# Two-layer transformer block, float32: long convolutions by transforms at odd frequencies, even and odd samples apart, with the upper half of the filter products on GpSimd

## Chip, cores and metric

One core of a Trainium2 chip. The time is device microseconds of one execution; before and after are compared by the median of runs. The engines: TensorE (PE in the profile, its weight loads PEld), VectorE (DVE), ScalarE (ACT), GpSimd (POOL), SyncE (SP), which only issues DMAs here. SBUF is the on-chip memory that all engines read, PSUM the memory into which TensorE writes.

## What is computed

A diffusion transformer of width 1024 on 256 latent tokens (x) and 256 context tokens (ctx), in float32. Two layers, each: feed-forward, mixer, feed-forward, every one behind a norm whose scale and shift come from a modulation (a product of the conditioning vector with a large matrix, `mod_w`). The first layer's mixer has two halves of 512 channels: differential attention, and a Hyena branch with two long convolutions. The second layer's mixer is neighbourhood attention. The change is in the Hyena branch:

```
def long_conv_bidir(v, h_fwd, h_bwd, skip):
    n = v.shape[1]
    taps = jnp.concatenate([h_fwd, jnp.zeros_like(h_fwd[:1]), h_bwd[:0:-1]], axis=0)
    taps_f = jnp.fft.rfft(taps.astype(jnp.float32), n=2 * n, axis=0)
    v_f = jnp.fft.rfft(v.astype(jnp.float32), n=2 * n, axis=1)
    y = jnp.fft.irfft(v_f * taps_f[None], n=2 * n, axis=1)[:, :n]
    return (y + v.astype(jnp.float32) * skip.astype(jnp.float32)).astype(v.dtype)
...
    z = x1 * long_conv_bidir(v, filt[:, 0, 0], filt[:, 0, 1], hy_b[0])
    z = x2 * long_conv_bidir(z, filt[:, 1, 0], filt[:, 1, 1], hy_b[1])
```

n is 256 and there are 512 channels. The branch runs for both streams, latent and context, with the same filters. The filters come from a small network of the position and a window.

## The kernel before

All activations are kept transposed, channels on partitions, 512 tokens wide (latent, then context). A float32 operand is split into a high and a low part (`split`, lines 154 to 157: ScalarE writes the high part, line 156, VectorE or GpSimd the low one, line 157), and a product is three matmuls (`mm3`, lines 159 to 162). So 160, 161, 162 are the lines of nearly all products, 156 and 157 those of nearly all splits; tiles are told apart by name.

The order of a run, with the times of the profile:

- To 64.7 us: loads, the first modulations on TensorE (`mod_group`, lines 247 to 274, weights `mw`, products at line 264, result `modT` at line 238), and the filters. `filter_taps` makes the windowed taps of a convolution as sums and differences of the two directions (`flt`). `filter_spectra` multiplies them with tables of cosines and sines: for each half `f` of the 256 frequencies a real and an imaginary part, each over two blocks of 128 taps; for the lower half there is a third product, for the frequency 256, which shares a row with the sine's frequency 0. ScalarE scales and copies the results, which go to memory (`TR`, `TI`, `TN`).
- 64.7 to 455 us: the first feed-forward. Its first block (`ffn_first`, `products`) needs the weights' splits (`wh`, `wl`) and the normed tokens `h`, which `Adaln.stream` makes: VectorE `xr` (line 487), ScalarE the high part (line 488), VectorE the low one (line 489). Its four results take all four tiles of the PSUM pool that the filters' spectra use too.
- 455 to about 706 us: the first mixer. Projections, attention heads (`head`), the Hyena inputs (`emit_hy`, with the short convolution and a transposition by line 779; v and x1 go to memory by tokens), per-head norms (`norms`), and the long convolutions, from 632 us. `spectrum` multiplies a stream's tokens (`vy`) with cosines and sines, two halves of the frequencies with a real and an imaginary part over two blocks of tokens: 24 matmuls of 512 columns. VectorE multiplies the results with the filter's parts (lines 824, 825), adds (line 826) and splits (`y`). `tn` takes the place of the real filter part in one product of the lower half. `conv1` goes back to tokens (24 matmuls), multiplies with x1 (line 843) and writes the result, `hz`, to memory, from where `load_tokens` takes it for the second convolution. `conv2` goes back to channels (48 matmuls of 256 columns for each stream) and multiplies with x2 (line 861).
- Then the output projection (`out_project`), over the attention's rows first (`za`), then over the convolution's (`zb`); a gated sum into the residual ends each product (line 515). Then the second feed-forward, and the second layer, to 1931 us.

The order on each engine is not that of the code: the framework's planner puts an instruction forward when its operands and buffers would be free, with the order of the code as the priority. So the profile has products of the attention's rows (`pd<-z`) between those of the convolutions, although they stand behind them in the code. Within an engine the order is then fixed.

Pools that the change touches: `fp`, three tiles for window, tables and filter parts; `tp`, ten tiles `T` of [128, 512]; `xp`, six tiles `X` of [128, 256], for norms, rotary embedding and x2. Filter parts are loaded by `load_filters` (lines 789 to 793) on SP's queue.

Of the kernel before, what the change touches and what calls it, by code (L numbers as in the profile page):

```python
# [10 lines left out]
F32 = mybir.dt.float32  # L11
# [7 lines left out]
P = 128  # L19
# [18 lines left out]
# columns of the small table of constants  # L38
_CO = {}
_n = 0  # L40
for _name, _w in (("ident", 128), ("sel", 8), ("row", 63), ("wf", 3), ("mask", 64)):
    _CO[_name] = slice(_n, _n + _w)
    _n += _w
# [3 lines left out]
def constants():  # L47
    """Tables that depend on shapes alone."""
# [11 lines left out]
    wf = np.full((P, 3), 2.0 / 512)  # L60
    wf[0] = 1.0 / 512, 2.0 / 512, 0.0
    cst[:, _CO["wf"]] = wf
    # Columns in reach of each query's column, in the order of the shifted bias (row 63 - c).
# [19 lines left out]
    # big: FC [2 chunks of 256], FS, FS^T, window [2 chunks of 512]  # L83
    tf = np.outer(np.arange(n), np.arange(n)) % 512
    th = tf * (2.0 * math.pi / 512)
    fc = np.cos(th)
    fs = -np.sin(th)
    fs[:, 0] = (-1.0) ** np.arange(n)
# [4 lines left out]
    rows = lambda m: m.reshape(2, P, -1).transpose(1, 0, 2).reshape(P, -1)  # L93
    dft = np.concatenate([rows(fc), rows(fs), rows(fs.T)], 1).astype(f32)
    return {"cst": cst, "rope": rope, "tmp": tmp, "dft": dft, "win": rows(win).astype(f32)}


class _K:
    """The state of the kernel being built."""
# [3 lines left out]
def tile_dit(ctx: ExitStack, tc: tile.TileContext, a: dict, out: bass.AP, dbg=None):  # L103
# [11 lines left out]
    xp = ctx.enter_context(tc.tile_pool(name="xp", bufs=6))  # L115
# [6 lines left out]
    # Pairs of [128, 512]: the two parts of a split operand, or two plain tiles.  # L122
# [31 lines left out]
    def split(hi, lo, src, eng=V):  # L154
        """src = hi + lo, each of 12 bits."""
        S.activation(hi, src, AF.Copy)  # L156
        eng.tensor_tensor(lo, src, hi.bitcast(F32), op=ALU.subtract)  # L157
# [12 lines left out]
    wf = cst[:, _CO["wf"]]  # L170
# [14 lines left out]
    # silu of the conditioning in two of 32 columns, which two is up to where a slice begins  # L185
# [39 lines left out]
    res = [big.tile([P, TOK], F32, name=f"res{d}") for d in range(NDC)]  # L225
# [9 lines left out]
    def mod_finish(l, batch, sums):  # L235
        """The bias, and from (chunk of a half, half, stream) to (half, chunk of a half, stream)."""
# [10 lines left out]
    def mod_group(l, batch, i, g):  # L247
        """A quarter of index i of a layer's modulation, on the tensor engine: 512 columns, half of the rows.
# [889 lines left out]
```

## Time and profile before

| | |
|---|---|
| runs | 1937.55, 1932.49, 1934.93 us, median 1934.93 us |
| span of the profiled execution, first to last instruction | 1931.2 us (no other time is listed for it) |
| TensorE matmul | 1880.6 us busy, 97% |
| TensorE weight loads | 1586.8 us, 82% |
| VectorE | 1253.9 us, 65% |
| ScalarE | 740.3 us, 38% |
| GpSimd | 72.3 us, 4% |
| granted TensorE clock, mean | 0.992 |

How to read what follows: a row of the timeline has the start in us, the duration in us, engine, line, operation, output and inputs by the program's names, shape and number; in brackets the idle time of the engine before it and what ended it. A row of the groups has line, engine, operation, names, shapes and number, then busy us, mean ns of one, idle us before and what ended that. Matmuls overlap, so that their pace is the distance of their starts and not their duration.

### The profile page before, as it was taken

The page shows a single profiled execution, that of the slowest core. Times are in us where ns is not written, and L with a number is a line of the kernel's source. Part 1 is how long each engine was busy: PE and PEld are TensorE (multiplying, and loading weights), DVE is VectorE, ACT ScalarE, POOL GpSimd, SP SyncE. Part 2 cuts the span into 40 slices and gives each one's busy share as a digit, 9 for nine tenths or more (in the row PEclk, how much of TensorE's full clock was granted, in tenths as well). Part 3 has the DMA queues.
Part 4 walks back from the last instruction along what each step waited for, and adds up shares of the span by engine and source line. Part 5 has one row for each costly group of instructions (what it writes and reads, how often), then busy time and mean ns, then how long its engine had stood idle before and what let it go on. Part 6 is the DMA issues. An engine that isn't in the chain of part 4 may idle for free.

```text
span 1931.2 us, 26004 instructions
## 1 busy us (share of the span) xinstructions
PE 1880.6 (97%) x10486; PEld 1586.8 (82%) x10486; DVE 1253.9 (65%) x1948; ACT 740.3 (38%) x1199; POOL 72.3 (4%) x63
## 2 busy tenths in 40 slices
PE   7999999999999999999999999999999999989998
PEld 3878788889877788888888888878889888889998
DVE  5557686666666785976775467763445654576665
ACT  4533233224556234232233242321233555554443
POOL 1000000000100001000000200000000000120000
PEclk9999999999999999999999999999999999989999
DMA  7674555451332322654464224642232333325552
GB/s 260 216 243 171 190 181 196 134 191 30 113 120 77 120 82 80 236 196 153 144 218 161 88 77 163 207 154 84 89 119 84 96 82 80 67 91 193 196 169 73
DMA packets 191153, 271.73 MB, mean 141 GB/s; under 512 B 19703, under 2 KB 139898, under 8 KB 191032
## 3 DMA queue, kind: packets, MB, share of 16 engines
q1 hardware_dynamic: 189468, 267.69, 42.5%
q10 hardware_dynamic: 1260, 2.14, 0.3%
q8 instruction: 82, 1.34, 0.3%
q14 instruction: 39, 0.32, 0.0%
q0 software_dynamic: 304, 0.24, 0.0%
HBM read 262.69 MB, written 7.34 MB: 140 GB/s over the span
## 4 chain that ended last, share of the span: by engine, by line
PE 57%; issue 11%; DVE 3%; DMA 2%; ACT 1%; POOL 1%; SPq 0%; POOLq 0%; DVEq 0%; ACTq 0%
PE pu L160 10%; PE pu L161 10%; PE pu L162 10%; PE pd L160 6%; PE pd L162 6%; PE pd L161 6%; PE ps L160 2%; PE ps L162 2%; PE ps L161 2%; DMA bias<-in_na_rpb_dram 2%; PE ps L672 1%; DVE wl L157 1%; DVE acc L444 1%; PE ps L298 1%; ACT wh L156 0%
## 5 line engine op out<-in xcount | busy, mean ns | idle before, releaser
L162 PE MATMUL pu<-h,wl 128*128 128x512 f32 (+1 forms) x1600 | 544.8, 341 | 3.0 <-POOL wl L157 3.0
L160 PE MATMUL pu<-h,wh 128*128 128x512 f32 (+1 forms) x1600 | 544.4, 342 | 1.8 <-ACT h L488 1.5
L161 PE MATMUL pu<-h,wh 128*128 128x512 f32 (+1 forms) x1600 | 545.4, 341 | 0.1
L156 ACT ACTIVATE wh<-raw 128x1024 fp32r<-128x1024 f32 x228 | 240.6, 1059 | 544.8 <-PE pu L161 417.2
L157 DVE TENSOR_TENSOR wl<-raw,wh 128x1024 fp32r<-128x1024 f32 x216 | 263.0, 1222 | 179.6 <-ACT wh L156 175.3
L160 PEld LDWEIGHTS pu<-h,wh 128*128 128x128 f32 x1600 | 303.1, 190 | 44.5 <-issue 4.2
L162 PEld LDWEIGHTS pu<-h,wl 128*128 128x128 f32 x1600 | 304.0, 190 | 38.5 <-POOL wl L157 3.2
L161 PEld LDWEIGHTS pu<-h,wh 128*128 128x128 f32 x1600 | 304.3, 190 | 34.2 <-DVE h L489 0.7
L287 DVE SCALAR_TENSOR_TENSOR mv<-mw,sF,mv 128x1024 f32<-128x1024 f32 x210 | 258.5, 1279 | 20.9 <-DMA mw<-in_mod_w_dram 20.8
L156 ACT ACTIVATE w<-raw 128x1024 fp32r<-128x1024 f32 x88 | 91.5, 1056 | 163.1 <-PE ps L161 123.4
L552 DVE TENSOR_TENSOR sg<-sg,pu 128x512 f32<-128x512 f32 (+1 forms) x87 | 52.2, 603 | 134.7 <-PE pu L162 127.1
L515 DVE SCALAR_TENSOR_TENSOR res<-pd,gate,res 128x256 f32<-128x256 f32 x244 | 110.9, 478 | 39.8 <-PE pd L162 39.3
L157 DVE TENSOR_TENSOR w<-raw,w 128x1024 fp32r<-128x1024 f32 x88 | 106.9, 1220 | 41.5 <-ACT w L156 41.5
L160 PE MATMUL pd<-g,w 128*128 128x512 f32 (+1 forms) x376 | 133.2, 354 | 0.0
L162 PE MATMUL pd<-g,w 128*128 128x512 f32 (+1 forms) x376 | 132.4, 352 | 0.0
L161 PE MATMUL pd<-g,w 128*128 128x512 f32 (+1 forms) x376 | 132.2, 352 | 0.0
L160 PE MATMUL ps<-g,w 128*128 128x512 f32 (+1 forms) x320 | 116.2, 363 | 0.0
L162 PE MATMUL ps<-g,w 128*128 128x512 f32 (+1 forms) x320 | 116.0, 363 | 0.0
L161 PE MATMUL ps<-g,w 128*128 128x512 f32 (+1 forms) x320 | 116.0, 363 | 0.0
L162 PE MATMUL pd<-h,wl 128*128 128x512 f32 (+1 forms) x288 | 108.2, 376 | 1.6 <-DVE wl L157 1.6
L160 PE MATMUL pd<-h,wh 128*128 128x512 f32 (+1 forms) x288 | 108.6, 377 | 0.0
L161 PE MATMUL pd<-h,wh 128*128 128x512 f32 (+1 forms) x288 | 107.5, 373 | 0.0
(261 smaller groups left out, 2808.6 us busy)
## 6 DMA issues: line engine op xcount, KB each, us to landing
raw<-in_ffn_w_dram SPq DMA_DIRECT2D x132, 1024.0 KB, 5.4
mw<-in_mod_w_dram SPq DMA_DIRECT2D x144, 512.0 KB, 5.9
raw<-in_ab_w_in_dram SPq DMA_DIRECT2D x12, 1024.0 KB, 6.8
raw<-in_na_w_in_dram SPq DMA_DIRECT2D x12, 1024.0 KB
raw<-in_ab_w_out_dram SPq DMA_DIRECT2D x4, 1024.0 KB
raw<-in_na_w_out_dram SPq DMA_DIRECT2D x4, 1024.0 KB
bias<-in_na_rpb_dram SPq DMA_DIRECT2D x32, 96.0 KB, 6.1
dftr<-const_dft_dram SPq DMA_DIRECT2D x5, 256.0 KB
```

The lines of the kernel that those rows point to most:

```text
L156: S.activation(hi, src, AF.Copy)
L157: eng.tensor_tensor(lo, src, hi.bitcast(F32), op=ALU.subtract)
L160: nc.tensor.matmul(ps, wh, xh, start=start, stop=False)
L161: nc.tensor.matmul(ps, wh, xl, start=False, stop=False)
L162: nc.tensor.matmul(ps, wl, xh, start=False, stop=stop)
L287: V.scalar_tensor_tensor(acc, mw, c, acc, op0=ALU.mult, op1=ALU.add)
L298: nc.tensor.matmul(ps[32 * j : 32 * j + 32], row[:, 31 - b : 63 - b], mod_acc[l, i][j % 2][:, j // 2], start=b == 0, stop=b == len(batch) ...
L444: V.tensor_tensor(acc, acc, q, op=ALU.add)
L515: V.scalar_tensor_tensor(res[d][:, sl], ps[:, po], g[:, d, s : s + 1], res[d][:, sl], op0=ALU.mult, op1=ALU.add)
L552: V.tensor_tensor(sg[:, sl], sg[:, sl], p3[:, sl], op=ALU.mult)
L672: nc.tensor.transpose(at[kt // 2][:, o : o + P], e[:, P * kt : P * kt + P], ident)
```

## The change

The transforms are taken at 128 odd frequencies, 2k + 1 of 1024, instead of the 257 whole ones. At the mirrored frequency 512 - (2k + 1), the even samples give the same product as at 2k + 1 and the odd samples the negative one (for the sine the other way round). So a transform is one product over the 128 even samples, `e`, and one over the 128 odd ones, `o`; their sum is the spectrum at the lower frequency, their difference that at the mirrored one (`butterfly`). ScalarE copies `o` from PSUM, VectorE adds and subtracts. There is no frequency of its own kind left, so `TN` and `tn` go. Taps, v and x1 are taken in the order even, odd: a matmul's weights or a transposition read every second column.

In `spectrum`, the products with the filter are four for each half; those of the upper half, `f` = 1, go to GpSimd. For the first convolution the two halves are then combined, so that `conv1` needs one product over 128 frequencies for the even and one for the odd tokens: 12 matmuls instead of 24. `conv1` splits its result straight into the tiles of the second convolution instead of writing it to memory. `conv2` keeps its 48 matmuls and un-shuffles the tokens in its product with x2. Filter parts are loaded on GpSimd's queue. `xp` has five tiles instead of six. The window carries the scale 1/256, and the tables have three pieces in all, one of which the filters need, instead of two.

```
-    xp = ctx.enter_context(tc.tile_pool(name="xp", bufs=6))
+    xp = ctx.enter_context(tc.tile_pool(name="xp", bufs=5))
...
+    at = np.concatenate([np.arange(0, n, 2), np.arange(1, n, 2)])
+    th = np.outer(at, 2 * np.arange(P) + 1) % 1024 * (2.0 * math.pi / 1024)
+    fc, fs = np.cos(th), -np.sin(th)
...
-                nc.tensor.matmul(ps, hid[:, LAT * q + P * t : LAT * q + P * t + P], wo[o], start=True, stop=True)
+                nc.tensor.matmul(ps, hid[:, LAT * q + t : LAT * q + LAT : 2], wo[o], start=True, stop=True)
...
+    def butterfly(psum, tab, ev, od):
+        (th, tl), (e, o) = tab, (psum(), psum())
+        mm3(o, th[:, 1], tl[:, 1], *od, True, True)
+        mm3(e, th[:, 0], tl[:, 0], *ev, True, True)
+        x, y = T(name="bo"), T(name="bs")
+        S.activation(x, o, AF.Copy)
+        V.tensor_tensor(y, e, x, op=ALU.add)
+        return e, x, y
+
+    def filter_spectra(o, parts, psum, tab):
+        tabs = [[x.rearrange("p (i t f) -> p i t f", i=2, t=2)[:, i] for x in tab] for i in range(2)]
+        for i in parts:
+            e, x, y = butterfly(psum, tabs[i], *taps[o][i])
+            if i == 0:
+                V.tensor_tensor(x, e, x, op=ALU.subtract)
+            else:
+                V.tensor_tensor(x, x, e, op=ALU.subtract)
+            for f, v in enumerate((y, x)):
+                nc.scalar.dma_start((TR, TI)[i][o][f], v)
...
-                    nc.tensor.transpose(pst[:, P * t : P * t + P], y[:, P * t : P * t + P], ident)
+                    nc.tensor.transpose(pst[:, P * t : P * t + P], y[:, LAT * (t // 2) + t % 2 : LAT * (t // 2) + LAT : 2], ident)
...
-                nc.sync.dma_start(tf[o, f][0], TR[o][f])
-                nc.sync.dma_start(tf[o, f][1], TI[o][f])
+                nc.gpsimd.dma_start(tf[o, f][0], TR[o][f])
+                nc.gpsimd.dma_start(tf[o, f][1], TI[o][f])
...
+            xr, xi = [butterfly(psum, tabs[i], *[[x[:, t] for x in sp_] for t in range(2)]) for i in range(2)]
+            V.tensor_tensor(xr[1], xr[0], xr[1], op=ALU.subtract)
+            V.tensor_tensor(xi[1], xi[1], xi[0], op=ALU.subtract)
+            ys = []
             for f in range(2):
...
+                (tr, ti), r, i = tf[o, f], (xr[2], xr[1])[f], (xi[2], xi[1])[f]
+                eng = (V, nc.gpsimd)[f]
+                u1, u2 = T(name="u1"), T(name="u2")
+                eng.tensor_tensor(u1, r, tr, op=ALU.mult)
+                eng.tensor_tensor(u2, i, ti, op=ALU.mult)
+                eng.tensor_tensor(r, r, ti, op=ALU.mult)
+                eng.tensor_tensor(i, i, tr, op=ALU.mult)
+                V.tensor_tensor(u1, u1, u2, op=ALU.subtract)
+                V.tensor_tensor(r, r, i, op=ALU.add)
+                ys += [u1, r]
+            if o == 0:
+                rl, il, rh, ih = ys
+                c, d = T(name="c"), T(name="d")
+                V.tensor_tensor(c, rl, rh, op=ALU.add)
+                V.tensor_tensor(d, il, ih, op=ALU.subtract)
+                V.tensor_tensor(rl, rl, rh, op=ALU.subtract)
+                V.tensor_tensor(il, il, ih, op=ALU.add)
+                ys = [c, d, rl, il]
+            y = spectra[o, s] = [(G, H)[s](name="y") for _ in range(4)]
+            for g, x in zip(y, ys):
+                split(*g, x)
...
         def conv1(s, pinv=PS):
...
+            sp_ = tokens["hz", s] = [mp.tile([P, 2, TOK], F32R, tag="m", name="vy") for _ in range(2)]
             for t in range(2):
                 sl = slice(P * t, P * t + P)
                 ps = pinv()
-                for f in range(2):
-                    mm3(ps, th[0][:, f, sl], tl[0][:, f, sl], *y[f][0], f == 0, False)
-                    mm3(ps, th[2][:, f, sl], tl[2][:, f, sl], *y[f][1], False, f == 1)
+                for i in range(2):
+                    mm3(ps, inv[0][i][0][:, sl], inv[0][i][1][:, sl], *y[2 * t + i], i == 0, i == 1)
                 x = T(name="hx")
                 nc.sync.dma_start(x, VX["hx"][2 * s + t])
                 V.tensor_tensor(x, x, ps, op=ALU.mult)
-                nc.sync.dma_start(VX["hz"][2 * s + t], x)
+                split(sp_[0][:, t], sp_[1][:, t], x)
...
         def conv2(s, pinv=PS):
...
-                V.tensor_tensor(x, x, ps[:, :LAT], op=ALU.mult)
+                x3 = x.rearrange("p (a t) -> p a t", t=2)
+                V.tensor_tensor(x3, x3, ps[:, :LAT].rearrange("p (t a) -> p a t", t=2), op=ALU.mult)
```

More of the change, by code (lines that the diff above doesn't have):

```diff
@@ L40 @@
 _n = 0
-for _name, _w in (("ident", 128), ("sel", 8), ("row", 63), ("wf", 3), ("mask", 64)):
+for _name, _w in (("ident", 128), ("sel", 8), ("row", 63), ("mask", 64)):
     _CO[_name] = slice(_n, _n + _w)
@@ L59, in constants @@
     cst[:, _CO["row"]] = np.arange(63) == 31
-    wf = np.full((P, 3), 2.0 / 512)
-    wf[0] = 1.0 / 512, 2.0 / 512, 0.0
-    cst[:, _CO["wf"]] = wf
     c = 63 - np.arange(64)
@@ L92, in constants @@
     win = np.exp((-t[:, None] * deltas[None]).astype(f32).astype(np.float64))
-    rows = lambda m: m.reshape(2, P, -1).transpose(1, 0, 2).reshape(P, -1)
-    dft = np.concatenate([rows(fc), rows(fs), rows(fs.T)], 1).astype(f32)
-    return {"cst": cst, "rope": rope, "tmp": tmp, "dft": dft, "win": rows(win).astype(f32)}
+    return {"cst": cst, "rope": rope, "tmp": tmp, "dft": dft, "win": halves(win[at] / 256).astype(f32)}
 class _K:
+    pass
 @with_exitstack
@@ L331, in tile_dit @@
     TI = [[dr.tile([P, 512], F32, name=f"TI{o}{f}") for f in range(2)] for o in range(2)]
-    TN = [dr.tile([1, 512], F32, name=f"TN{o}") for o in range(2)]
     def load_x(s):
@@ L341, in load_x, with tables @@
             S.activation(res[d][:, LAT * s : LAT * s + LAT], pst[:, :LAT], AF.Copy)
-    def tables(n, hi, lo):
-        for i in range(n):
+    def tables(first, n, hi, lo):
+        for i in range(first, first + n):
             r = T(name="dftr")
@@ L359, in filter_tables @@
             nc.gpsimd.dma_start(skip[o][0:1], a["hy_bias"][0][o : o + 1])
-        tab = [pair(fp, "f", F32R, "tab") for _ in range(2)]
-        tables(2, lambda i: tab[i][0], lambda i: tab[i][1])
+        tab = pair(fp, "f", F32R, "tab")
+        tables(0, 1, lambda i: tab[0], lambda i: tab[1])
         return wo, [win[:, 0], win[:, 1]], skip, tab
@@ L758, in head @@
                 S.activation(oT[hd][:, LAT * s : LAT * s + LAT], po[:, :LAT], AF.Copy)
-        VX = {k: [dr.tile([P, TOK], F32, name=f"{k}{t}") for t in range(4)] for k in ("hv", "hx", "hz")}
+        VX = {k: [dr.tile([P, TOK], F32, name=f"{k}{t}") for t in range(4)] for k in ("hv", "hx")}
         X2 = [dr.tile([P, TOK], F32, name=f"X2{i}") for i in range(4)]
@@ L903, in mixer_ab @@
         tab = [wp.tile([P, 2, TOK], F32R, tag=("whi", "wlo", "wlo")[i], name="tab") for i in range(3)]
-        tables(3, lambda i: tab[i][:, 0], lambda i: tab[i][:, 1])
-        th, tl = [[t[:, x].rearrange("p (t f) -> p t f", t=2) for t in tab] for x in range(2)]
-        tn = pair(fp, "f", F32, "tn")
-        for o in range(2):
-            nc.sync.dma_start(tn[o][1:], TR[o][0][1:])
-            nc.sync.dma_start(tn[o][0:1], TN[o])
+        tables(0, 3, lambda i: tab[i][:, 0], lambda i: tab[i][:, 1])
+        tabs = [[tab[0][:, x].rearrange("p (i t f) -> p i t f", i=2, t=2)[:, i] for x in range(2)] for i in range(2)]
+        inv = [[[tab[1 + f][:, x, LAT * i : LAT * i + LAT] for x in range(2)] for i in range(2)] for f in range(2)]
         norms((0, 1))
```

58 lines of the change are left out of this document (6 added, 52 removed).

## The prediction

> **What bounds the kernel now.** I read the page first, then the busy times by stretch, then the order of time around the two places that the change touches: the filters' spectra (45 to 65 us) and the long convolutions (632 to 707 us). The page says what to look for:
>
> ```profile
> span 1931.2 us, 26004 instructions
> ...
> PE 1880.6 (97%) x10486; PEld 1586.8 (82%) x10486; DVE 1253.9 (65%) x1948; ACT 740.3 (38%) x1199; POOL 72.3 (4%) x63
> ```
>
> Over the whole span TensorE is the bound and GpSimd is idle, so fewer products and some elementwise work on GpSimd look like a plain gain. The stretches decide otherwise. The first row below is from the first filter product of the convolutions to the last split of their result, the second from there to the next norm; columns are stretch, its length, then busy time of PE, PEld, DVE, ACT, POOL.
>
> ```profile
> 632.40:706.70 74.30, 72.32 (x369) 61.24 (x369) 64.89 (x116) 22.83 (x39) 2.01 (x1) 0.98 0.31 103
> 706.70:728.40 21.70, 19.75 (x122) 17.66 (x121) 15.29 (x24) 5.99 (x11) 4.78 (x3) 1.00 0.31 97
> ```
>
> In the first, VectorE is busy 64.9 of 74.3 us. It is a second bound close behind TensorE: if TensorE's work vanished there, at most 74.3 - 64.9 = 9.4 us could be won. Most of that lies in one hole, where VectorE waits for the per-head norms (idle before each in brackets):
>
> ```profile
> 646.70 0.17 DVE L878 TENSOR_SCALAR rs<-ps 128x8 f32<-128x8 f32 x1 [2.60 <-PE ps L875]
> ...
> 650.93 0.75 DVE L886 SCALAR_TENSOR_TENSOR on<-oT,sub,ps 128x512 f32<-128x512 f32 x1 [3.47 <-PE ps L884]
> 652.64 0.75 DVE L886 SCALAR_TENSOR_TENSOR on<-oT,sub,ps 128x512 f32<-128x512 f32 x1 [0.96 <-PE ps L884]
> ```
>
> That is 2.60 + 3.47 + 0.96 = 7.0 us; behind it VectorE idles 2.4 us in 54.
>
> **Products removed.** The groups that read the tables, one of the three equal lines of a split product each:
>
> ```profile
> L160 PE MATMUL pu<-vy,tab x32: 387/389/398, 632.0 to 689.6; 128*128 128x512 f32 x32
> L160 PE MATMUL ps<-tab,y x32: 274/283/384, 676.2 to 703.3; 128*128 128x256 f32 x32
> L160 PE MATMUL pu<-flt,tab x20: 389/391/793, 44.9 to 64.1; 128*128 128x512 f32 x20
> L160 PE MATMUL ps<-y,tab x16: 389/389/497, 652.8 to 666.2; 128*128 128x512 f32 x16
> ```
>
> By the code, a filter spectrum goes from 30 to 12 products, so 60 to 24 for two (36 fewer); a stream's spectrum from 24 to 12, four times (48 fewer); the first convolution from 24 to 12, twice (24 fewer); the second keeps its 96. Their durations overlap; the pace is the distance of starts:
>
> ```profile
> 632.23 0.39 PE L161 MATMUL pu<-vy,tab 128*128 128x512 f32 x1
> 632.46 0.40 PE L162 MATMUL pu<-vy,tab 128*128 128x512 f32 x1
> ```
>
> 0.23 us. So 36 x 0.23 = 8.3 us of TensorE go in the filter stage and 72 x 0.23 = 16.6 us in the convolutions, 24.9 us in all. What is late next in each?
>
> **Filter stage, taken at -5.0 us (between -8.3 and -0.8).**
>
> ```profile
> 31.95 12.89 SPq L261 DMA_DIRECT2D mw<-in_mod_w_dram  x6
> ...
> DMA to landing us min/median/max: 5.6/6.8/7.9
> ...
> 52.43 1.05 PE L264 MATMUL ps<-mw,sF 128*32 128x512 f32 x4
> ...
> 55.28 0.25 DVE L238 TENSOR_TENSOR modT<-ps,modb 128x16 f32<-128x16 f32 x2 [7.20 <-PE ps L273]
> ...
> 60.41 0.88 DVE L489 SCALAR_TENSOR_TENSOR h<-xr,modT,h 128x256 fp32r<-128x256 f32 x2
> 61.20 3.49 DVE L157 TENSOR_TENSOR wl<-raw,wh 128x1024 fp32r<-128x1024 f32 x3
> ...
> 64.52 0.39 PE L162 MATMUL pu<-flt,tab 128*128 128x512 f32 x1
> 64.74 0.28 PE L160 MATMUL pu<-h,wh 128*128 128x256 f32 x1
> ```
>
> The last filter product at 64.52 is followed at once by the first of the ffn. Without 8.3 us of filters that one waits for data: the first lower half of h ends at 60.41 + 0.44 = 60.85, and that hangs on modT, on the last modulation group (52.43), on its weights, whose issue ends at 31.95 + 12.89 = 44.84. They land 6.8 us later (the median in this stretch), at 51.6, and one table of 256 KB fewer goes ahead of them, so the group can start about 1.1 us earlier: 60.85 - 1.1 = 59.7, a gain of 64.74 - 59.7 = 5.0 us. The change adds eight VectorE operations here (a sum and a difference for each of four butterflies), eight of 0.6 us (pace below) less one table's split: 4.2 us, which fit into the 7.20 us in which VectorE waits ahead of modT. If the second filter's come too late for that hole, all of it is paid in front of the ffn: -5.0 + 4.2 = -0.8. In the ffn behind TensorE is never idle, so what is won here stays won:
>
> ```profile
> 200.00:250.00 50.00, 50.00 (x220) 39.52 (x219) 36.02 (x45) 13.22 (x15) 0.00 (x0) 1.00 0.49 168
> ```
>
> **Convolutions, taken at +6.0 us.** First the operations: the splits and products of a stream's spectrum are 16 on VectorE now. In the change they are 4 for the butterflies, 8 products of which 4 go to GpSimd, 4 sums, 4 splits, and for the first convolution 4 combinations: 16 and 20 on VectorE, so 72 instead of 64.
>
> ```profile
> 636.68 0.68 DVE L826 TENSOR_TENSOR u<-u,u 128x512 f32<-128x512 f32 x1
> 637.28 0.68 DVE L825 TENSOR_TENSOR u<-pu,tn 128x512 f32<-128x512 f32 x1
> ```
>
> Pace 0.60 us, from SBUF as from PSUM: 8 x 0.60 = +4.8 us on VectorE although half of the upper products left it.
>
> Second the engine they went to. The trace has no 512-wide product on GpSimd, but these:
>
> ```profile
> 489.01 0.74 POOL L715 TENSOR_TENSOR u<-u,rope 128x256 f32<-128x256 f32 x1 [1.79 <-ACT qk L156]
> 713.01 2.39 POOL L157 TENSOR_TENSOR wl<-raw,wh 128x1024 fp32r<-128x1024 f32 x1 [64.06 <-ACT wh L156]
> 713.27 2.42 DVE L444 TENSOR_TENSOR acc<-acc,sq 128x256 f32<-128x256 f32 x1 [0.34 <-ACT sq L442]
> ...
> 716.57 0.42 DVE L444 TENSOR_TENSOR acc<-acc,sq 128x256 f32<-128x256 f32 x1
> ...
> 1084.20 2.40 POOL L157 TENSOR_TENSOR wl<-raw,wh 128x1024 fp32r<-128x1024 f32 x1 [18.05 <-ACT wh L156]
> 1084.96 0.88 DVE L515 SCALAR_TENSOR_TENSOR res<-pd,gate,res 128x256 f32<-128x256 f32 x2 [1.84 <-PE pd L162]
> ```
>
> On the line from 0.74 us at 256 to 2.39 at 1024, 512 wide is 0.74 + 1.65/3 = 1.29 us. Of more weight is the VectorE sum at 713.27: 0.42 us alone, 2.42 us while GpSimd works, and it ends 0.29 us behind GpSimd's. It reads two operands from SBUF. The two sums at 1084.96 read one from PSUM and run beside GpSimd at their usual 0.44 us. So a GpSimd product stops a VectorE operation with both operands in SBUF for (2.42 - 0.42)/2.39 = 0.84 of itself, here 1.08 us, and others not at all. That prices each of the 16 products between 0 and 1.08 us of VectorE. The Trainium skill says the same more strictly ("SBUF — State Buffer", Who interferes with whom): the read interface is locked for the whole instruction of whichever came first, and the other blocks fully; by that it would be 1.29 us each, and it speaks against this half of the change.
>
> Which value? In the new stage 56 of the 72 spectral operations read SBUF twice, with some 19 splits of other tiles; 16 butterfly operations read PSUM, and so do some 32 others (gated sums, products with a convolution's result). By count 75 of 123, by the spectral ones alone 56 of 72: 0.61 to 0.78 of 1.08 us. I take 0.7 us: 16 x 0.7 = +11.2 us.
>
> Third what gives time back. The hole of 7.0 us is filled, since the first spectrum's work on VectorE now lasts through it and the next stream's butterflies need little of TensorE: -7.0 (between 0 and -9.4). And the attention half of the output projection, which is in the same stretch as filler, can leave gated sums for the next stretch:
>
> ```profile
> L515 DVE SCALAR_TENSOR_TENSOR res<-pd,gate,res 128x256 f32<-128x256 f32 x15 | 6.9, 478 | 0.0
> ```
>
> 15 at a pace of 0.40 us are 6.0 us, and the next stretch has 21.70 - 15.29 = 6.4 us free; I take half, -3.0 (between 0 and -6.0). Sum: 4.8 + 11.2 - 7.0 - 3.0 = +6.0 us, where TensorE alone would have given -16.6. The bounds that go together are 4.8 + 0 - 9.4 - 6.0 = -10.6 and 4.8 + 17.3 = +22.1.
>
> **The rest, at nothing.**
>
> ```profile
> L156 ACT ACTIVATE vy<-hv 128x512 fp32r<-128x512 f32 x4 | 2.4, 624 | 2.2 <-DMA hv<-hz 2.2
> 80.08 3.52 SPq L909 DMA_DIRECT2D tn<-TN  x1
> L779 PE MATMUL ps<-cst,cv 128*128 128x128 f32 x32 | 5.0, 278 | 1.6 <-DVE cv L773 1.6
> L861 DVE TENSOR_TENSOR x<-x,ps 128x256 f32<-128x256 f32 x8 | 3.1, 413 | 0.0
> 55.69 2.07 DVE L487 SCALAR_TENSOR_TENSOR xr<-res,A,bs 128x256 f32<-128x256 f32 x5
> ```
>
> The round trip of hz through memory ends; ScalarE waited 2.2 us for it, beside a busy VectorE. The filter loads leave SP's queue for GpSimd's, and the four tn loads go (one held SP 3.52 us); nobody waits for them for hundreds of microseconds, except the second filter's last pair, whose tile is released by the first's last products; behind that wait on GpSimd's queue stand only the products that need it. Transposes, the filters' weight loads and the second convolution's products now step by two: nothing, or at worst their time again (5.0 and 3.1 us, the first under a bound TensorE). Five small tiles instead of six: VectorE wrote five in one go before; nothing. The per-head norms' power on GpSimd comes behind the first four products, up to 4 x 1.29 = 5.2 us later; only the filler waits for it. A TensorE that idles is also slowed (the third number from the right is the granted clock, 0.92 and 0.73 of full speed around an idle time of 1.85 us), but it has 74.30 - 72.32 + 16.6 = 18.6 us to spare:
>
> ```profile
> 645.00:650.00 5.00, 3.15 (x19) 2.58 (x18) 0.77 (x2) 0.00 (x0) 2.01 (x1) 0.92 0.31 105
> 650.00:655.00 5.00, 5.00 (x24) 4.59 (x23) 3.11 (x5) 1.26 (x2) 0.00 (x0) 0.73 0.00 0
> ```
>
> ScalarE gains eight copies of 0.6 us, 22.83 of 74.30 us busy.
>
> Sum: -5.0 + 6.0 = +1.0 us against the profiled execution. Its span is 1931.2 us, 3.7 less than the median 1934.93 of the runs, which I put down to what lies around it: 1935.9, said as 1936.
>
> **Rivals.** A measurement tells about 0.3%, 5.8 us. *The lock is paid in full* (slower): the two engines' products of a half become ready together and all read SBUF, so every GpSimd product blocks: 16 x 1.08 = 17.3. For it: the row at 713.27; against it: a third of VectorE's operations read PSUM. Convolutions 4.8 + 17.3 - 7.0 - 3.0 = +12.1; with the filter stage at -3.0, half its added sums exposed, +9 in all: 1944. It decides where the loss passes 1.0 us a product. *VectorE has enough to do beside GpSimd* (faster): PSUM operations fall into GpSimd's time and the loss is 0.15 us: 2.4. Then 4.8 + 2.4 - 9.4 - 6.0 = -8.2, with -5.0 in front -13.2: 1921.7. For it: port time, 56 + 19 operations of 0.6 (45 us) and 16 x 1.29 (21 us), fits into 74.3 us; against it: each engine goes in its own fixed order. *TensorE's whole 24.9 us* would need VectorE not to matter: 64.9 of 74.3 us excludes it.
>
> **Numbers.** Forecast, within 0.3%: 0.46. Faster rival 0.28, slower 0.26. With a loss of 0.4 to 1.0 us a product the forecast's own range is 1931 to 1941. The range of 8 in 10 cuts the far half of each rival's tail: 1923 to 1947.
>
> **What would show it.** The first ffn product near 59.7 us; the eight filter sums and differences inside VectorE's wait for modT; from the first butterfly to the last z split 76 to 84 us with TensorE busy some 56 and VectorE over 90%; GpSimd products of 1.2 to 2 us and beside them VectorE operations of 1.2 to 1.9 us. I am wrong if those stay at 0.7 us, if the stretch shortens below 70 us, or if the filter stage gives nothing.

## The result, and the profile after

| | before | after |
|---|---|---|
| median of the runs | 1936.24 us (1932.49 to 1938.17, 4 runs) | 1965.80 us (1961.52 to 1967.55, 4 runs) |
| ratio after / before, 95% interval | | 1.0149 [1.0133, 1.0165] |
| span of the profiled execution | 1931.2 us | 1964.6 us (its own time 1966.36 us) |
| granted TensorE clock, mean | 0.992 | 0.978 |

The change costs 1965.80 - 1936.24 = 29.6 us. The forecast was no change, and the upper end of the range 1947. The page of the changed kernel, first lines:

```profile
span 1964.6 us, 25826 instructions
...
PE 1874.9 (95%) x10378; PEld 1582.5 (81%) x10378; DVE 1284.5 (65%) x1963; ACT 740.0 (38%) x1200; POOL 104.3 (5%) x87
```

TensorE has 108 matmul records fewer, as the change says, and is busy 5.7 us less; VectorE is busy 30.6 us more with 15 instructions more; GpSimd 32.0 us more. So VectorE's instructions have become longer. Where the time went shows in two stretches, which are compared in every kernel from here on. **A** reaches from the first product of a spectrum (`pu<-vy`) to the end of the last split of a spectrum (`y`). **B** reaches from there to GpSimd's power in the next norm, that of the second feed-forward. Columns as in the prediction: stretch, its length, busy time of PE, PEld, DVE, ACT, POOL, granted clock, DMA share, GB/s. Before:

```profile
632.00:699.24 67.24, 65.26 (x322) 54.75 (x321) 57.83 (x99) 19.75 (x33) 2.01 (x1) 0.97 0.35 114
699.24:728.38 29.14, 27.20 (x171) 24.47 (x170) 22.75 (x42) 9.46 (x18) 4.76 (x2) 1.00 0.23 73
```

After:

```profile
635.19:711.37 76.18, 43.21 (x187) 36.21 (x186) 69.65 (x90) 21.93 (x37) 28.83 (x19) 0.77 0.16 52
711.37:755.65 44.28, 42.33 (x234) 37.04 (x234) 31.48 (x58) 11.59 (x21) 4.76 (x2) 0.97 0.23 72
```

A grew by 8.9 us and B by 15.1, together 24.1 us. In A TensorE now works 43 of 76 us, and VectorE 70: VectorE is the bound. In B it is the other way round: TensorE is busy 42.3 of 44.3 us, with 63 more products than before. The two profiled executions are 33.4 us apart, 3.8 more than the medians. Of the other 9.3 us, 6.1 lie behind B and are followed below (five tiles in `xp`). The remaining 3.2 lie ahead of A and are not put down to the change: A starts between 630.2 and 634.6 us in three kernels with the old code up to there, and between 631.4 and 635.6 in six with the new.

VectorE's part of A, by groups. First before, where 16 products of each kind take 0.68 us:

```profile
L824 DVE TENSOR_TENSOR u<-pu,tf 128x512 f32<-128x512 f32 x16 | 10.9, 683 | 0.6 <-PE pu L162 0.6
...
L515 DVE SCALAR_TENSOR_TENSOR res<-pd,gate,res 128x256 f32<-128x256 f32 x11 | 5.0, 478 | 0.0
```

After, the 16 lower products that stayed on VectorE:

```profile
L815 DVE TENSOR_TENSOR u<-bs,tf 128x512 f32<-128x512 f32 x4 | 7.1, 1768 | 0.0
L816 DVE TENSOR_TENSOR bs<-bs,tf 128x512 f32<-128x512 f32 x4 | 7.0, 1745 | 0.0
L817 DVE TENSOR_TENSOR bs<-bs,tf 128x512 f32<-128x512 f32 x4 | 7.0, 1744 | 0.0
...
L814 DVE TENSOR_TENSOR u<-bs,tf 128x512 f32<-128x512 f32 x4 | 5.4, 1350 | 0.0
```

They take 26.5 us instead of 16 x 0.68 = 10.9: 15.6 us more. Beside them the upper products on GpSimd, the first alone, the others in alternation:

```profile
640.18 1.29 POOL L814 TENSOR_TENSOR u<-bo,tf 128x512 f32<-128x512 f32 x1 [43.60 <-issue]
641.43 1.74 POOL L815 TENSOR_TENSOR u<-bo,tf 128x512 f32<-128x512 f32 x1
643.12 1.71 POOL L816 TENSOR_TENSOR bo<-bo,tf 128x512 f32<-128x512 f32 x1
```

The starts are 1.69 us apart, as long as VectorE's operations beside them: one pair of products each 1.7 us.

The group of gated sums (`L515` above, 11 of them in A before) does not occur in A after. The views of the tile `pd` say what hangs on that, before and after, for the gated sums (the last line of each fence) and the products with `z` that they end; the columns are number, shortest, middle and longest duration in ns, first and last start. Before:

```profile
L160 PE MATMUL pd<-z,wh x28: 389/389/486, 640.2 to 698.1; 128*128 128x512 f32 x28
...
L515 DVE SCALAR_TENSOR_TENSOR res<-pd,gate,res x32: 470/478/485, 665.0 to 742.9; 128x256 f32<-128x256 f32 x32
```

After:

```profile
L157 PE MATMUL pd<-z,wh x8: 389/390/390, 639.3 to 666.3; 128*128 128x512 f32 x8
...
L506 DVE SCALAR_TENSOR_TENSOR res<-pd,gate,res x29: 468/477/485, 712.0 to 754.5; 128x256 f32<-128x256 f32 x29
```

Before, the first gated sum starts at 665.0, and 28 + 27 + 27 = 82 products with `z` fill TensorE's waits all through A. After, it starts at 712.0, behind the end of A. Until its gated sums have read it, an accumulator `pd` is not free, so after 8 x 3 = 24 products, the last three from 666.3, the filler stops. The other 58 go to B, at a pace of 0.227 us 13.2 of the 15.1 us that B grew.

### The profile page after: what moved, and what is told of

It reads as the page before. It is cut to its first block, busy times and chain, and to the rows that moved or that the text cites. A ratio compares the mean times of both kernels' runs of the same rounds, so it can differ in the third digit from the quotient of the medians.

```text
span 1964.6 us, 25826 instructions
## 1 busy us (share of the span) xinstructions
PE 1874.9 (95%) x10378; PEld 1582.5 (81%) x10378; DVE 1284.5 (65%) x1963; ACT 740.0 (38%) x1200; POOL 104.3 (5%) x87
## 4 chain that ended last, share of the span: by engine, by line
PE 49%; issue 11%; DVE 5%; DMA 2%; ACT 2%; POOL 1%; SPq 0%; POOLq 0%; DVEq 0%; ACTq 0%
PE pu L157 9%; PE pu L158 9%; PE pu L159 8%; PE pd L157 5%; PE pd L159 5%; PE pd L158 4%; PE ps L157 2%; PE ps L159 2%; PE ps L158 2%; DMA bias<-in_na_rpb_dram 2%; DVE acc L435 1%; PE ps L663 1%; PE ps L294 1%; ACT wh L153 0%; DVE u L815 0%
```

## The experiments

All ratios are to the kernel before, measured beside it. "A", "B" and "z in A" (products with `z` issued within A) are from the profile of each kernel.

### The upper products back on VectorE

```
-                eng = (V, nc.gpsimd)[f]
+                eng = V
```

> The sixteen upper products go back from GpSimd to VectorE; the order of everything else stays. Theory A (the lock): a GpSimd product costs VectorE 1.07 us, so in the four spectra the stretches from VectorE's first product to its first difference, now 6.50, 6.16, 6.12 and 6.41 us (25.2 in all), become eight products at 0.60 each, 4.8 us, 19.2 in all: 6.0 us less, 1959.8 us. Rival (VectorE's products are long for a reason of their own: a filter part that comes late, a tile that is not free): the four lower ones stay at 1.7 us each and the four upper ones come on top, 16 x 0.60 = 9.6 us more, 1975 us.

Measured: 1959.35 us (1958.68 to 1960.24), ratio 1.0122 [1.0106, 1.0137].

```profile
633.85:704.33 70.48, 42.93 (x187) 36.00 (x186) 63.74 (x106) 21.94 (x37) 2.79 (x3) 0.77 0.17 56
704.33:748.62 44.29, 42.34 (x234) 36.90 (x233) 31.49 (x59) 11.60 (x21) 4.75 (x3) 0.98 0.23 72
```

With 16 instructions more, VectorE is busy 5.9 us less in A, and A is 5.7 us shorter; B stays. So the move to GpSimd costs, rather than brings, some 6 us: 32 products by VectorE alone take 32 x 0.60 = 19.2 us, and in the change the four phases from the first lower product to the first difference take 6.50 + 6.16 + 6.12 + 6.41 = 25.2. That is about a fifth of the loss; the other four fifths are still there, and so is the 44-us tail.

### The butterfly's sum left in PSUM

```
-        x, y = T(name="bo"), T(name="bs")
+        x, y = T(name="bo"), e if stay else T(name="bs")
...
-            V.tensor_tensor(xr[1], xr[0], xr[1], op=ALU.subtract)
-            V.tensor_tensor(xi[1], xi[1], xi[0], op=ALU.subtract)
+            V.scalar_tensor_tensor(xr[1], xr[1], -2.0, xr[0], op0=ALU.mult, op1=ALU.add)
+            V.scalar_tensor_tensor(xi[1], xi[1], 2.0, xi[0], op0=ALU.mult, op1=ALU.subtract)
...
-                eng.tensor_tensor(r, r, ti, op=ALU.mult)
-                eng.tensor_tensor(i, i, tr, op=ALU.mult)
+                r_, i_ = (r, i) if f else (T(name="u3"), T(name="u4"))
+                eng.tensor_tensor(r_, r, ti, op=ALU.mult)
+                eng.tensor_tensor(i_, i, tr, op=ALU.mult)
```

> The butterfly's sum, the lower half, stays in PSUM, so that each of VectorE's lower products reads one operand from PSUM and one from SBUF beside GpSimd's products; as many operations as in the changed kernel. Theory A in its narrow form (only a VectorE operation with both operands in SBUF is stopped): VectorE's sixteen lower products fall from 1.67 to 0.60 us and GpSimd's from 1.7 to 1.29; then VectorE waits for GpSimd's four, so that a spectrum takes 5.2 us from the first product instead of 6.3: about 4 us less, 1962 us. Wide form (GpSimd stops any VectorE operation): 1.67 and 1.7 as they are, 1966 us.

Measured: 1959.51 us (1958.27 to 1963.55), ratio 1.0128 [1.0109, 1.0147], A 69.0, B 48.1. VectorE's timeline, a difference, a lower product, then two operations on two SBUF tiles, while GpSimd multiplies:

```profile
661.07 0.69 DVE L808 SCALAR_TENSOR_TENSOR bo<-bo,pu 128x512 f32<-128x512 f32 x1
...
663.47 0.69 DVE L818 TENSOR_TENSOR u<-pu,tf 128x512 f32<-128x512 f32 x1
664.06 1.26 DVE L819 TENSOR_TENSOR u<-u,u 128x512 f32<-128x512 f32 x1
665.24 1.75 DVE L820 TENSOR_TENSOR u<-u,u 128x512 f32<-128x512 f32 x1
```

and GpSimd's in the same time:

```profile
663.49 1.28 POOL L817 TENSOR_TENSOR bo<-bo,tf 128x512 f32<-128x512 f32 x1
664.73 1.72 POOL L818 TENSOR_TENSOR bo<-bo,tf 128x512 f32<-128x512 f32 x1
```

With one operand in PSUM the product takes 0.69 us beside a GpSimd product of 1.28. The very next operations read SBUF twice and take 1.26 and 1.75. So what blocks is a second SBUF operand, and not GpSimd being at work. The Trainium skill ("SBUF — State Buffer", Who interferes with whom) states the same condition: with at most one SBUF input, outside its 2-port modes, VectorE does not contend with GpSimd; with two it contends with a GpSimd instruction that reads SBUF. Of the 7.2 us that A lost, B took 3.8 back. That leaves 3.4 us, although the median is 6.3 lower: in the profile the rest lies ahead of A, where this edit changes nothing.

### The output projection's attention half moved ahead

`out_project(wout, range(4), za, ...)` and its gates from behind `conv2(1)` to directly behind `norms((2, 3))`, so that its products and gated sums come before the convolutions in the order of priority.

> The attention half of the output projection stands ahead of the first convolution in the code instead of behind the second, so its gated sums stand between VectorE's spectral work again. Theory B (held back): in the changed kernel they stood behind all of it, the two accumulators of PSUM stayed full, and three quarters of that half's products, 16 us of TensorE, ran behind the convolutions. From the last split of the convolutions' result to the next norm it is 32.6 us now and was 21.7 before: it falls to about 22. VectorE gets up to 16 x 0.40 = 6.4 us more in the convolutions, some of it in its holes of 6.6 us. Together 4.5 to 10.9 us less: 1955 to 1961 us. Rival (VectorE alone sets the end, TensorE's tail is hidden behind it): the 6.4 us move from one stretch to the other and the time stays, 1966 us.

Measured: 1959.20 us (1957.58 to 1961.99), ratio 1.0122 [1.0107, 1.0137].

```profile
632.17:715.96 83.79, 57.11 (x259) 47.59 (x258) 77.90 (x109) 25.10 (x40) 27.72 (x19) 0.83 0.17 55
715.96:750.00 34.04, 30.18 (x162) 25.55 (x162) 21.51 (x40) 8.49 (x18) 4.76 (x3) 0.86 0.24 74
```

96 products with `z` are in A now, and B falls by 10.3 us. But the gated sums need VectorE, and A grows by 7.6: a net gain of 2.7 us there. (The next norm, measured between its powers on GpSimd, is 19.65 us instead of 22.26.) Filler that ends on VectorE is no free filler when VectorE is the bound.

### The filters' products issued twice

```
-        mm3(o, th[:, 1], tl[:, 1], *od, True, True)
-        mm3(e, th[:, 0], tl[:, 0], *ev, True, True)
+        for _ in range(times):
+            mm3(o, th[:, 1], tl[:, 1], *od, True, True)
+            mm3(e, th[:, 0], tl[:, 0], *ev, True, True)
```

with `times` = 2 for the filters: 24 products more, 24 x 0.23 = 5.5 us.

> The filters' spectra issue each of their products twice (the second overwrites the first with the same result): 24 products, 5.4 us of TensorE, put back of the 8.3 that the change removed. Theory C: the products removed there were cover for VectorE, which prepares the first feed-forward's operands until 68.5 us in both kernels; without them TensorE idled 4.8 us and then ran at half the clock until 68.4. So putting them back costs nothing: the 96th product of the feed-forward, at 76.6 us now and 76.1 before, stays within 1 us, and if the clock stays up it may come up to 3 us earlier; 1963 to 1967 us. Rival (TensorE bounds this stage and the gain was lost elsewhere): 5.4 us later, 1971 us.

Measured: 1964.84 us (1963.47 to 1967.67), ratio 1.0151 [1.0136, 1.0167], the same as the change without them. So TensorE's products do not set the end of the filter stage, and those that the change removed there brought nothing. What sets it is seen in the changed kernel itself, in TensorE's timeline (in brackets the idle time before):

```profile
57.66 0.39 PE L157 MATMUL pu<-h,wh 128*128 128x256 f32 x1 [1.20 <-ACT h L479]
61.24 0.39 PE L158 MATMUL pu<-h,wh 128*128 128x256 f32 x1 [3.19 <-DVE h L480]
```

and in its stretches around that wait:

```profile
60.00:64.00 4.00, 2.76 (x13) 2.62 (x13) 4.00 (x6) 2.53 (x4) 1.30 (x4) 0.72 0.78 264
64.00:68.00 4.00, 2.77 (x13) 2.56 (x13) 4.00 (x9) 1.31 (x3) 0.87 (x2) 0.50 0.82 261
68.00:72.00 4.00, 4.00 (x33) 4.00 (x33) 3.96 (x10) 1.02 (x3) 0.00 (x0) 0.93 1.07 363
```

The first ffn product starts at 57.66, 7.1 us earlier than before, the second only at 61.24. The first needs the high part of `h` alone, the second the low one, from VectorE:

```profile
58.97 0.69 DVE L411 TENSOR_TENSOR bs<-pu,bo 128x512 f32<-128x512 f32 x1 [1.24 <-DMA TR<-bs]
...
60.71 0.88 DVE L480 SCALAR_TENSOR_TENSOR h<-xr,modT,h 128x256 fp32r<-128x256 f32 x2
```

VectorE stood still for 1.24 us, by the profile until an earlier filter sum had been written to memory, and then did the next sum. So the first low part of `h` ends at 60.71 + 0.44 = 61.15, 0.3 us later than before (60.85). From 60 to 72 us VectorE is busy 11.96 of 12 us; it prepares `h` and the low parts of the weights, as it did before. The last of the eight low parts of `h` for the first stream,

```profile
67.28 1.28 DVE L480 SCALAR_TENSOR_TENSOR h<-xr,modT,h 128x256 fp32r<-128x256 f32 x3
```

ends at 68.56; the kernel before has at the same place:

```profile
67.77 0.88 DVE L489 SCALAR_TENSOR_TENSOR h<-xr,modT,h 128x256 fp32r<-128x256 f32 x2
```

which ends at 68.65. The 96th product of the ffn starts at 76.61 after, 76.14 before, and at 75.52 with the doubled products. One profile each would not tell a difference of 1 us, but the others agree: in the nine profiles with the change's code in this stage the 96th starts between 72.25 and 78.14, in the four with the code of before between 73.83 and 76.14. Behind the idle time the granted clock is 0.72 and 0.50 of full speed up to 68 us, although TensorE is busy 69% of that time. The Trainium skill ("TensorE: Matmul & The Clock Gate", What's actually happening) has half speed after at least one idle window of about 3.4 us; the row agrees that idle time is followed by half speed, here behind waits of 1.20 and 3.19 us.

### The kernel before, with five tiles in xp

```
-    xp = ctx.enter_context(tc.tile_pool(name="xp", bufs=6))
+    xp = ctx.enter_context(tc.tile_pool(name="xp", bufs=5))
```

> The kernel before with one edit of the change alone, five small tiles X instead of six. Theory D: it is what the second layer lost in stretches whose code the change does not touch; between the adaptive norms' powers these are 14.51 us before and 15.56 after, 222.63 and 223.59, 199.14 and 200.66, together 3.5 us: 1939.7 us, with those three stretches as after. Rival (the lower clock or the other order behind the convolutions carries over): the three stretches as before, 1936.2 us.

Measured: 1940.06 us (8 runs), before 1935.79 (12 runs), ratio 1.0023 [1.0013, 1.0033]: 4.3 us. The norms show where. The powers on GpSimd of the second feed-forward's norm, one for each stream, before:

```profile
728.38 0.69 POOL L452 TENSOR_TENSOR rs<-rs,nhalf 128x2 f32<-128x2 f32 x1 [7.57 <-DVE rs L451]
...
748.31 0.69 POOL L452 TENSOR_TENSOR rs<-rs,nhalf 128x2 f32<-128x2 f32 x1
```

With five tiles:

```profile
730.97 0.70 POOL L452 TENSOR_TENSOR rs<-rs,nhalf 128x2 f32<-128x2 f32 x1 [7.55 <-DVE rs L451]
...
753.22 0.70 POOL L452 TENSOR_TENSOR rs<-rs,nhalf 128x2 f32<-128x2 f32 x1 [3.33 <-DVE rs L451]
```

19.93 us have become 22.25, and the first such distance in the second layer went from 14.51 to 15.58. The changed kernel has 22.26 and 15.56. A and B are 67.24 and 29.15 us here, as before, so the loss lies wholly behind them: 7.0 us between the profiled executions, where the change has 6.1. The first distance is not tied to the five tiles alone: the kernel with the projection ahead also has five and shows 19.65. The changed kernel with six tiles was not tried.

### The norms' statistics ahead of the first spectrum

```
+        rs23 = norms_rs((2, 3))
...  (the first spectrum)
-        norms((2, 3))
+        norms((2, 3), rs23)
```

`norms_rs` holds the part of `norms` up to the power, so that the hole at the norms has work beside it.

> The changed kernel with the per-head norms of heads 2 and 3 in two parts: sums and power ahead of the first spectrum in the code, the scaling behind it as it was. Theory E (the hole): in the changed kernel VectorE stands still for 0.82 + 3.88 + 0.96 = 5.7 us behind the first spectrum for the sums, the power on GpSimd and the broadcast; with these done beside the spectrum the hole goes and VectorE's chain is 5.7 us shorter: 1960 us. Rival (the next spectrum's and the convolution's products come no sooner, so VectorE waits for those instead): 1965 us.

Measured: 1962.05 us (1958.81 to 1962.38), ratio 1.0134 [1.0119, 1.0148], A 73.3, B 43.7. A lost 2.9 us; the median is 3.75 below that of the change, between the two expectations. VectorE's idle time in A falls from 76.18 - 69.65 = 6.5 to 73.30 - 69.48 = 3.8 us: the hole is real, and what of it is filled is won, in A.

### The last three together

The PSUM form, the projection moved ahead, and the norms' statistics ahead.

> Three edits together: lower half in PSUM, attention half of the output projection ahead of the first convolution, norms of heads 2 and 3 in two parts. If lock, held-back projection and hole are three separate terms of one chain: -6.3 - 6.6 - 5.7 = -18.6, 1947 us; the gated sums read PSUM and can run while GpSimd multiplies, up to 4 us more, 1943 us. If they are the same VectorE time counted twice or three times: 1953 us or above.

Measured: 1954.55 us (1953.80 to 1955.05), ratio 1.0098 [1.0084, 1.0112].

```profile
630.24:702.95 72.71, 57.17 (x259) 47.55 (x258) 70.22 (x109) 24.85 (x40) 25.19 (x19) 0.87 0.19 64
702.95:736.57 33.62, 29.59 (x162) 25.07 (x161) 21.52 (x40) 8.50 (x18) 4.77 (x2) 0.87 0.25 75
```

A and B together are 106.3 us, 14.1 less than in the change and 9.9 more than before. Of these 9.9, A has 5.5, with VectorE busy 70.2 us instead of 57.8, and B 4.5, with a granted clock of 0.87 instead of 1.00. The gain in the median is 11.3, where the three alone gave 6.3 + 6.6 + 3.75 = 16.6. By A and B it is the other way round: alone they took 3.3 + 2.6 + 3.4 = 9.4 us off, together 14.1. There the moves help each other, while the second layer's mixer, which none of them touches, took 229.9 us instead of 223.6. VectorE is busy 70.2 of 72.7 us in A: nothing is left to reorder there, only instructions to take out.

### The upper products on VectorE, with the other two moves

> The same with all filter products on VectorE instead of the lower half in PSUM. Separate terms: -6.5 - 6.6 - 5.7 = -18.8, 1947 us, of which the 16 products more on VectorE are 9.6 us that GpSimd could still take. Counted twice: 1953 us or above.

Measured: 1961.93 us (1960.86 to 1962.31), ratio 1.0136 [1.0120, 1.0152], A 76.7, B 33.5. A and B together fell by 4.5 us against the first experiment, but the median rose by 2.6. The spans show part of it outside: the second layer's mixer, from norm to norm, is 226.7 us instead of 223.7, and the way from the first to the second norm of the first layer 424.7 instead of 422.7. That a change in the first layer moves those is not explained (below).

### Without the combinations of the halves

```
-                c, d = T(name="c"), T(name="d")
-                V.tensor_tensor(c, rl, rh, op=ALU.add)
-                ...
-                ys = [c, d, rl, il]
+                ys = [rl, il, rh, ih]
```

> The changed kernel without the four combinations of the first convolution's spectrum for each stream (its halves go into the first convolution as they are, so that sums and differences of them are left out of the computation): eight VectorE operations fewer, nothing else. Theory A (VectorE's chain sets the end of the convolutions): 8 x 0.60 = 4.8 us less or a little more, since the first convolution can start with the first split: 1959 to 1961 us. Rival (TensorE, or the latency from engine to engine, sets it): 1964 to 1966 us.

Measured: 1969.45 us (1967.24 to 1972.05), ratio 1.0166 [1.0150, 1.0182]: slower than the change, where one theory said faster and the other at most the same. A is 72.2, 4.0 shorter for eight operations of 0.60 us, as it should be; but B is 49.0, 4.7 longer, with 24 products with `z` in A still. The gain was given back in the tail, whole:

```profile
704.39:753.35 48.96, 46.21 (x242) 41.27 (x243) 31.86 (x58) 11.59 (x21) 4.76 (x2) 0.90 0.20 65
```

TensorE has 242 products there instead of the change's 234, and a granted clock of 0.90 instead of 0.97. The second layer's mixer is 228.3 instead of 223.6 us besides.

### The spectra's transforms issued twice

The edit of the filters' products, for the spectra of the streams: 48 products more, 10.9 us.

> Each product of the spectra's transforms is issued twice (the second overwrites the first with the same result), 48 in the convolutions and none in the filters: 10.9 us of the TensorE time that the change removed comes back. Theory A: TensorE stands idle for some 35 of the 120 us from 635 to 755, and VectorE sets the end: 0 to 2 us more, 1966 to 1968 us. Rival (the removed products do shorten the chain, and the loss would be larger with them): up to 10.9 us more, 1977 us.

Measured: 1972.35 us (1970.82 to 1974.09), ratio 1.0181 [1.0166, 1.0195], A 77.9, B 46.5, so 6.6 us over the change, for 10.9 us of work, although TensorE had 33 us without work in A. In the profiled executions, which are 4.4 us apart, A is 1.7 us longer and B 2.2; the remaining 2.6 us of the median have no place in the two stretches. Neither theory is right: the products are neither hidden nor paid in full.

### Two tries on the kernel before

The norms' statistics ahead, in the kernel before:

> The kernel before with the norms of heads 2 and 3 in two parts, as above. There VectorE's hole is 7.0 us, but TensorE is busy 72.3 of the 74.3 us, at clocks of 0.92 and 0.73 around the one idle time. Theory: only TensorE's idle time and its lowered clock can be won, 2.0 to 3.4 us: 1933 us. Rival (the products are only put elsewhere): 1936 us.

Measured: 1935.10 us (12 runs), before 1937.26 (18 runs), ratio 0.9990 [0.9981, 0.9999], A 62.5, B 33.7. The hole goes and A falls by 4.7 us; 72 instead of 82 products with `z` are in A, and B takes 4.6 back. It has the lowest ratio of all kernels here, but at 0.1%, with an interval that ends at 0.9999, it can hardly be told from the kernel before.

GpSimd for the sums and differences (line 826) in the kernel before, whose products read PSUM:

```
-                    V.tensor_tensor(u1, u1, u2, op=op)
+                    nc.gpsimd.tensor_tensor(u1, u1, u2, op=op)
```

> The kernel before with its sixteen sums and differences of filter products on GpSimd instead of VectorE: both operands in SBUF, while VectorE's own products beside them read PSUM. Theory A in its narrow form: VectorE's products stay at 0.60 us beside GpSimd and only its splits are stopped; VectorE gets 9.6 us less work, but TensorE bounds that stage: 1934 to 1938 us. Wide form (any VectorE operation is stopped): 16 x 1.07 - 9.6 = 7.5 us more work on VectorE, and the products of the next half wait for it: 1940 us or above.

Measured: 1943.38 us (1942.05 to 1946.13, 7 runs), ratio 1.0031 [1.0020, 1.0043].

```profile
630.24:698.12 67.88, 61.61 (x284) 49.74 (x282) 48.17 (x76) 18.04 (x33) 22.41 (x17) 0.92 0.30 97
698.12:737.09 38.97, 36.97 (x207) 32.92 (x208) 26.84 (x49) 11.14 (x19) 4.77 (x3) 0.96 0.26 81
```

GpSimd's timeline:

```profile
634.54 2.58 POOL L826 TENSOR_TENSOR u<-u,u 128x512 f32<-128x512 f32 x2 [43.03 <-DVE u L825]
```

and VectorE's at the same time:

```profile
634.92 0.68 DVE L825 TENSOR_TENSOR u<-pu,tn 128x512 f32<-128x512 f32 x1
636.53 1.14 DVE L157 TENSOR_TENSOR y<-u,y 128x512 fp32r<-128x512 f32 x1 [0.93 <-ACT y L156]
```

The products keep 0.68 us, only a split of two SBUF tiles becomes longer, and VectorE is busy 9.7 us less in A than before. Yet A is not shorter: eight of its splits now wait for the high part behind the slower engine, 7.2 us in all (0.93 here), where one waited 0.8 before. And 48 instead of 82 products with `z` are in A: B is 9.8 us longer. Here there is hardly a lock, VectorE is relieved, and the loss is in the tail all the same.

| kernel | ratio | A, us | B, us | z in A |
|---|---|---|---|---|
| before | 1 | 67.2 | 29.1 | 82 |
| after | 1.0149 | 76.2 | 44.3 | 24 |
| upper products on VectorE | 1.0122 | 70.5 | 44.3 | 24 |
| sum in PSUM | 1.0128 | 69.0 | 48.1 | 24 |
| projection ahead | 1.0122 | 83.8 | 34.0 | 96 |
| filters' products twice | 1.0151 | 76.6 | 44.3 | 24 |
| before, five tiles in `xp` | 1.0023 | 67.2 | 29.1 | 82 |
| norms' statistics ahead | 1.0134 | 73.3 | 43.7 | 24 |
| last three together | 1.0098 | 72.7 | 33.6 | 96 |
| upper on VectorE, other two moves | 1.0136 | 76.7 | 33.5 | 96 |
| without the combinations | 1.0166 | 72.2 | 49.0 | 24 |
| spectra's transforms twice | 1.0181 | 77.9 | 46.5 | 24 |
| before, norms' statistics ahead | 0.9990 | 62.5 | 33.7 | 72 |
| before, sums on GpSimd | 1.0031 | 67.9 | 39.0 | 48 |

## Why the prediction was wrong

It named the right engine and the right lock, and still missed by 30 us, because it took work that leaves a stretch for work that is gone. The terms, one by one:

**Time given back by deferral, predicted -3.0: the step that failed.** "The attention half of the output projection, which is in the same stretch as filler, can leave gated sums for the next stretch", and VectorE had 6.4 us free there. The sums did leave, with other work: by the groups of A, 11 gated sums (a pace of 0.40 us), two splits of weights (1.2 us each) and four smaller operations are gone, 8.2 us. But a gated sum holds an accumulator, so the products behind it leave too: 58 of them, 13.2 us, into a stretch where TensorE is the bound (27.20 of 29.14 us before). The prediction looked at VectorE's free time in the next stretch and not at TensorE's, though the row that it quoted shows TensorE at 19.75 of 21.70 us. -3.0 became B's +15.1. The 18.6 us that it gave TensorE to spare overlook the same thing: such time is of use only to work that may be issued then. That the products hang on the gated sums is shown by the counts: with 0, 5, 9, 11 and 16 gated sums in A, the kernels have 24, 48, 72, 82 and 96 products with `z` in it, since two sums free an accumulator for twelve. The tail follows these counts in the main: 24 go with a B of 44 to 49 us, 48 with 39, 72 with 34 and 82 with 29. It does not follow at the end: 96 go with 34 again. There, with the projection ahead, TensorE has 162 products in B instead of 171 and is still busy 30.2 us instead of 27.2, at a granted clock of 0.86 instead of 1.00. That undoing it alone wins little is shown by the projection moved ahead: then VectorE pays in A.

**The lock, predicted 16 x 0.7 = +11.2.** The mechanism was right, the size too small. The four phases take 25.2 us instead of 16 x 0.60 = 9.6: 15.6, or 0.97 a product; in full alternation, where the starts are 1.67 apart, it is 1.07, the upper bound of 1.08 that the prediction had from one row. It took less on the count of operations that read PSUM, but the four products of a half are all ready at once on both engines and meet each other in a row; the operations on PSUM stand elsewhere in VectorE's order. The rival that the lock is paid in full named this, gave 1944, and did not see the tail either.

**Eight operations more, predicted +4.8.** The kernel without the combinations, eight operations too, has A 4.0 shorter. Right, as far as A goes.

**The hole at the norms, predicted -7.0.** It stayed:

```profile
655.09 0.17 DVE L879 TENSOR_SCALAR rs<-ps 128x8 f32<-128x8 f32 x1 [0.82 <-PE ps L876]
...
659.14 0.75 DVE L887 SCALAR_TENSOR_TENSOR on<-oT,sub,ps 128x512 f32<-128x512 f32 x1 [3.88 <-PE ps L885]
660.85 0.75 DVE L887 SCALAR_TENSOR_TENSOR on<-oT,sub,ps 128x512 f32<-128x512 f32 x1 [0.96 <-PE ps L885]
```

0.82 + 3.88 + 0.96 = 5.7 instead of 7.0. The first spectrum's longer work did not last through it: in VectorE's order it stands ahead of the norm's steps, at 653.59 its last split starts, and between 655.09 and 660.85 there are only the norm's own steps, each of which waits for another engine. Moving the statistics ahead filled half of it.

With these, A adds up: 15.6 + 4.8 more of spectral work, 8.2 of other work that left, and VectorE's idle time down from 67.24 - 57.83 = 9.4 to 6.5 us, 2.9 less: 15.6 + 4.8 - 8.2 - 2.9 = 9.3 against the measured 8.9. The forecast's own stretch, to the last `z` split, came to 87.9 us, where 76 to 84 were named.

**Filter stage, predicted -5.0.** It gave nothing. The forecast let the first ffn product wait for the first low part of `h` and moved that from 60.85 to 59.7 us; it came at 61.15. Of the eight filter sums and differences that were to fit ahead of `modT`, three did; five came behind it, one of them with the wait of 1.24 us for a write to memory ahead of `h`. The prediction's own weak end, -0.8, was for this case. The product at 57.66 needs the high part alone, and 3.19 us of waiting follow it. Besides, "in the ffn behind TensorE is never idle, so what is won here stays won" was wrong for the first 10 us: VectorE makes the first stream's low parts of `h` until 68.6 us in both kernels. The first consumer's start was taken for the end of the stage.

**Five tiles in `xp`, predicted nothing.** 4.3 us in the kernel before. The prediction looked at the one place where the diff moves work (five tiles written in one go) and not at the norms, which use the same pool.

24.1 for A and B, from the profiles, and 4.3 for `xp`, from medians, are 28.4 of the measured 29.6; the rest is within the interval, which is 3 us either way. Against the forecast the terms are off by 15.1 (the tail), 5.0 (filters), 4.4 (lock), 4.1 (hole) and 4.3 (`xp`), less 5.2 us of work that left A beyond the 3.0 foreseen: 27.7 of the 28.6 us by which the change of 29.6 missed the forecast +1.0. The forecast of "no change" rested on two gains, -5.0 and -10.0. The first did not come; the second did, as 8.2 + 2.9 = 11.1 us in A, and was paid back with 15.1 in B.

**What stays open.** Part of the differences between the experiments lies where no edit touched anything. The second layer's mixer took 222.6 us before, 223.6 after, and 226.3 to 229.9 in four of the experiments, where TensorE waits longer for the high parts of the bias (`bh`), 3.6 to 6.0 us instead of 2.4 to 3.2. Why was not found, and it blurs medians by some us: so the edits are judged by A and B first. Nor was it settled why the products issued twice in the spectra cost 6.6 us and not nothing, or why the kernel without the combinations was left with more products and a lower clock in B. Both kernels show only that in A and B a change on one engine alone moves little.

## What to carry to other kernels

Before work is moved to a second engine or out of a stretch, follow what it ends: an operation that frees an accumulator carries its products with it, and if the next stretch is bound by TensorE they are paid there in full. Price two engines on shared operands by the rows where both work in a burst, and look at which operands lie in PSUM. And when a stage is made shorter on one engine, look for the time at which the last input of the next stage is ready, not the first.

## What the runs showed of the hardware

VectorE and GpSimd, each with two 512-wide float32 operands in SBUF, take turns: 1.67 to 1.69 us for one product of each, where VectorE alone has a pace of 0.60 us and GpSimd alone takes 1.28 us. That is far more than 1.28 and only 0.2 us less than 0.60 + 1.28 = 1.88, so an alternation has little overlap. Both engines show the whole turn as their own busy time, 1.75 and 1.71 us, so busy shares overstate what either does. With one operand in PSUM the pair runs side by side at 0.69 and 1.28 us.

The granted clock was 0.72 from 60 to 64 us and 0.50 from 64 to 68, behind waits of 1.20 and 3.19 us, with TensorE at work 69% of these 8 us; in A of the changed kernel, with TensorE busy 43.2 of 76.2 us, it was 0.77 on the mean.
